# Norm weights folded into the rotation tables, and one reciprocal for both row sums of a query tile

## The chip, the cores and the metric

The kernel runs on one core of one Trainium2 chip. The metric is the device time of one execution in microseconds (us); smaller is better. A core has five engines, each of which works through its own instruction list in order: TensorE (PE in the profile, with PEld for its weight loads), VectorE (DVE), ScalarE (ACT), GpSimd (POOL) and SyncE (SP). DMA transfers are issued by an instruction on one of these lists and then run beside them.

## What is computed

The reference is a trunk of two layers. The first has MLA attention beside chunked retention, the second has differential attention beside bidirectional RWKV-7 time mixing; a gated ConvFFN follows each. 512 latent tokens and 128 context tokens go through it, 640 in all, with 256 cached context keys. The change touches only the second layer's differential attention, 4 heads with two maps each:

```python
q = rms_norm(dq.reshape(b, n, DIFF_HEADS, 2, DIFF_DH), qn)   # qn, kn: 64 weights each
k = rms_norm(dk.reshape(b, n, DIFF_HEADS, 2, DIFF_DH), kn)
q, k = apply_rope(q, cos, sin), apply_rope(k, cos, sin)      # latent tokens only
...
s = jnp.einsum('bqhcd,bkhcd->bchqk', qi, k) * scale          # scale = 0.125
p = jax.nn.softmax(s, axis=-1)
w = p[:, 0] - lam * p[:, 1]
o = jnp.einsum('bhqk,bkhe->bqhe', w, v)                      # then an rms_norm over each head
```

`rms_norm(x, g)` is x / sqrt(mean(x^2) + eps) * g, and `apply_rope` turns pairs of neighbouring columns by an angle that depends on the token. The normed k of the 128 context tokens, which are not rotated, is an output too.

## The kernel before

All five instruction lists are made ahead of the run by a scheduler: it takes the program in the order in which the Python code emits it, estimates how long each instruction takes, and puts the instructions of each engine into a fixed order by those estimates (L2112). An engine never overtakes: an instruction that waits holds everything behind it on its list. So a small change in the code can move rows that it does not name.

The stage that the change touches runs from about 1050 to 1510 us. There `rwkv_scan` (L1649) emits the RWKV work piece by piece and, in between, single steps of a background generator, `side_mix` (L1404); `weave` and `Side` (L211 and after) set how many steps go between two pieces, and tie a step's matmuls to earlier RWKV matmuls. The background generator runs two things in turn.

`odd_qkv` (L1266) projects q, k and v. Six groups of 256 columns (two for q, two for k, two for v) times five token tiles of 128 make 30 tiles; each takes 16 matmuls (L1326), after which ACT copies the result into `raw` (L1331) and, for q and k, squares it into `m` (L1334), and DVE sums the squares per head (L1335). PSUM has two `qkv` buffers. While one group is projected, `post` (L1278) of the group before it runs: for each tile, DVE multiplies `raw` by 1/rms (L1288, one operand is `y`, the result of the square root), POOL multiplies it by the norm weights (L1289, operand `rt`), DVE multiplies it by the cosine half of the rotation table into `m` (L1294), POOL by the sine half into another `m` (L1295), DVE adds the two into `raw` (L1298, two instructions), PE turns the tile (L1304, `qtr`), ACT and DVE split it into a high and a low part in the one `pt` buffer (L440, L444), and two DMAs write that to the arrays `dq` or `dk` (L1308). The fifth tile, the context, is not rotated. The table `ropd` (128 x 512, 256 KB) is loaded once, from ACT's list.

`diff_attn` (L1409) then takes the heads one by one. `load` (L1412) brings q, k and v of a head in with DMAs that POOL issues (L1424 to L1429, `aq`, `ak`, `ac`, `av`). `s1` (L1435) makes, for each of 5 query tiles and both maps, the scores on PE (L1442, `sc`), their maximum on DVE (L1445, `mx`) and the exponentials with their row sum on ACT (L1447, `p` and `sm`). From the two sums DVE makes two reciprocals (L1452 `rr`, L1453 `so`) and one product (L1454), and then the weights p0 + rr * p1 (L1455); dividing by p0's sum is put off. `s2` (L1459) turns the weights (L1466, copied by ACT at L1467), multiplies them with v (L1471), copies the result out (L1472) and squares it on ACT (L1473), which is scaled by `so` there. `finish` (L1476) norms a finished head.

Of the kernel before, what the change touches and what calls it, by code (L numbers as in the profile page):

```python
# [9 lines left out]
F32 = mybir.dt.float32  # L10
# [3 lines left out]
OP = mybir.AluOpType  # L14
# [248 lines left out]
class Trunk:  # L263
# [1002 lines left out]
    def odd_qkv(self, D):  # L1266

        nc, a = self.nc, self.a
        with self.pool("qk", 1, "left") as qp, self.psum("qps", 2) as qps, self.psum("qtr") as qtr:
            def tile(s, w, bufs, dt=F32):  # L1270
                return qp.tile([128, w], dt, name=self.nm(s), tag=s, bufs=bufs)

            nc.vector.tensor_scalar(self.row("dqn"), self.row("dqn"), 0.125, None, op0=OP.mult)
            rope = qp.tile([128, 2, 4, 64], F32, name="ropd")
            nc.scalar.dma_start(rope.rearrange("p a t d -> p (a t d)"), a["ropd"])
            h = self.x

            def post(g, raw, ms):  # L1278
                nc.vector.tensor_scalar(ms, ms, 1.0 / 64, EPS, op0=OP.mult, op1=OP.add)
                r = self.rsqrt(ms, 20)  # L1280
                yield
                name, gain = (("q", "dqn"), ("k", "dkn"))[g // 2]
                gain = self.row(gain)
                c0 = (g % 2) * 256
                for t in range(5):
                    q = raw[t]
                    qv = q.rearrange("p (h d) -> p h d", h=4)
                    nc.vector.tensor_tensor(qv, qv, r[:, t * 4:t * 4 + 4, None].to_broadcast([128, 4, 64]), op=OP.mult)  # L1288
                    nc.gpsimd.tensor_tensor(qv, qv, gain[:, None, :].to_broadcast([128, 4, 64]), op=OP.mult)  # L1289
                    yield  # L1290
                    if t < 4:
                        m1, m2 = tile("m", 256, 3), tile("m", 256, 3)
                        v1, v2 = (m.rearrange("p (h d) -> p h d", h=4) for m in (m1, m2))
                        nc.vector.tensor_tensor(v1, qv, rope[:, 0, t:t + 1, :].to_broadcast([128, 4, 64]), op=OP.mult)  # L1294
                        nc.gpsimd.tensor_tensor(v2, qv, rope[:, 1, t:t + 1, :].to_broadcast([128, 4, 64]), op=OP.mult)  # L1295
                        yield
                        for e in range(2):
                            nc.vector.tensor_tensor(q[:, e::2], m1[:, e::2], m2[:, 1 - e::2], op=OP.add)  # L1298
                    elif name == "k":
                        nc.sync.dma_start(a["dk_o"][:, c0:c0 + 256], q)  # L1300
                    yield
                    pt = qtr.tile([128, 512], F32, name=self.nm("qtr"), tag="tr")
                    for i in range(2):
                        nc.tensor.transpose(pt[:, i * 128:i * 128 + 128], q[:, i * 128:i * 128 + 128], self.ident)  # L1304
                    pts = tile("pt", 512, 1, F32R).rearrange("p (n x) -> p n x", n=2)
                    self.split_to(pts[:, 0], pts[:, 1], pt[:, :256])
                    for c in range(2):
                        nc.sync.dma_start(D[name][g % 2, c, :, :, t].rearrange("y d k -> d y k"),  # L1308
                                          pts[64 * c:64 * c + 64].bitcast(F32).rearrange("p n (h k) -> p (n h) k", h=2))
                    yield  # L1310

            def load(g):
                w = [tile("w", 1024, 3) for _ in range(2)]
                for i in range(2):
                    nc.sync.dma_start(w[i], a["wb_tm"][g][:, i * 1024:i * 1024 + 1024])
                return w

            w, pp = load(0), iter(())
            for g in range(6):
                wn = load(g + 1) if g < 5 else None  # L1320
                raw = []
                ms = self.S("ms", 20) if g < 4 else None
                for t in range(5):
                    ps = qps.tile([128, 512], F32, name=self.nm("qkv"), tag="ps")[:, :256]
                    for k in range(8):
                        nc.tensor.matmul(ps, h[k][:, t * 128:t * 128 + 128], w[k // 4][:, k % 4 * 256:k % 4 * 256 + 256], start=k == 0, stop=k == 7)  # L1326
                        if k % 2:
                            next(pp, None)
                            yield
                    r = tile("raw", 256, 6)  # L1330
                    nc.scalar.copy(r, ps)  # L1331
                    if g < 4:
                        sq = tile("m", 256, 3)
                        nc.scalar.activation(sq, ps, AF.Square)  # L1334
                        nc.vector.tensor_reduce(ms[:, t * 4:t * 4 + 4], sq.rearrange("p (h d) -> p h d", h=4), axis=AX.X, op=OP.add)  # L1335
                        raw.append(r)
                    else:
                        cs = slice((g - 4) * 256, (g - 4) * 256 + 256)
                        nc.sync.dma_start(D["v"][t][:, cs], r)
                        if t == 4:  # L1340
                            nc.sync.dma_start(a["dv_o"][:, cs], r)
                for _ in pp:
                    yield
                pp = post(g, raw, ms) if g < 4 else iter(())
                w = wn
            kc = tile("w", 1024, 3)
            ks = [tile("w", 1024, 3, F32R) for _ in range(2)]
            nc.sync.dma_start(kc, a["dkc"])
            self.split_to(*ks, kc)
            for i in range(2):  # L1350
                for c in range(2):
                    for g in range(2):
                        nc.sync.dma_start(D["k"][g, c, 2 * i:2 * i + 2, :, 5:7].rearrange("h d t k -> d h (t k)"),
                                          ks[i][64 * c:64 * c + 64, g * 512:g * 512 + 512].bitcast(F32).rearrange("p (h x) -> p h x", h=2))
            yield
# [53 lines left out]
    def diff_attn(self, D, ap, scp, trp):  # L1409
        nc, a = self.nc, self.a  # L1410
        nlam = self.diff_lam(ap)
# [23 lines left out]
        def s1(q, k, qt, so):  # L1435
            n = 768 if qt < 4 else 128
            pr = []
            for c in range(2):
                sc = scp.tile([128, 1024], F32, name=self.nm("sc"), tag="sc")
                for o, w, t0, t1 in ((0, 0, 0, 4), (512, 1, 0, 2)) if qt < 4 else ((0, 0, 4, 5),):  # L1440
                    for i in range(2):
                        nc.tensor.matmul(sc[:, o:o + (t1 - t0) * 128], q[c][i][:, qt].bitcast(F32R), k[c][w][:, t0:t1].bitcast(F32R), start=i == 0, stop=i == 1)  # L1442
                yield
                mx, sm = self.S("mx", 1), self.S("sm", 1)
                nc.vector.tensor_reduce(mx, sc[:, :n], axis=AX.X, op=OP.max, negate=True)  # L1445
                p = ap.tile([128, 768], F32, name=self.nm("p"), tag="p", bufs=4)[:, :n]
                nc.scalar.activation(p, sc[:, :n], AF.Exp, bias=mx, accum_out=sm)  # L1447
                pr.append((p, sm))
                yield
            (p0, m0), (p1, m1) = pr  # L1450
            r = self.S("rr", 1)
            nc.vector.reciprocal(r, m1)  # L1452
            nc.vector.reciprocal(so, m0)  # L1453
            nc.vector.scalar_tensor_tensor(r, r, nlam, m0, op0=OP.mult, op1=OP.mult)  # L1454
            nc.vector.scalar_tensor_tensor(p0, p1, r, p0, op0=OP.mult, op1=OP.add)  # L1455
            yield
            return p0
# [18 lines left out]
        def finish(h, o, so, ms):  # L1476
            nc.vector.tensor_scalar(ms, ms, 1.0 / 128, EPS, op0=OP.mult, op1=OP.add)
            f = self.rsqrt(ms, 5)
            nc.vector.tensor_tensor(f, f, so, op=OP.mult)
            yield  # L1480
            on = self.X("on")
            for t in range(5):
# [13 lines left out]
        prev = None  # L1496
        for h in range(4):
            q, k, v = load(h)
            o = self.X("ao").rearrange("p (t c) -> p t c", t=5)
            so, ms = self.S("so", 5, "so"), self.S("oms", 5, "oms")  # L1500
            yield
            for qt in range(5):
                w = yield from s1(q, k, qt, so[:, qt:qt + 1])
                if prev:
                    yield from s2(*prev[0])
                    if prev[1]:
                        yield from finish(*prev[1])
                prev = ((w, v, qt, o[:, qt], so[:, qt:qt + 1], ms[:, qt:qt + 1]), (h, o, so, ms) if qt == 4 else None)
        yield from s2(*prev[0])
        yield from finish(*prev[1])  # L1510

# [604 lines left out]
```

## Time and profile before

| | |
|---|---|
| median of 3 runs | 2064.08 us (2053.91 to 2064.95) |
| the profiled execution: its time | 2061.5 us |
| the profiled execution: its span | 2059.7 us, 36835 instructions |
| busy, share of the span | PE 95%, PEld 86%, DVE 61%, ACT 43%, POOL 9% |
| stage with the change | about 1050 to 1510 us of the span |

The profile is one execution. Its span runs from the first to the last instruction, and its time adds what lies around that. An engine's busy share is an average over stages that have different limits, so a stage is read by itself: which engine is busy in it, at what clock TensorE ran (1.00 in a window is full speed, 2.4 GHz; 0.50 is the lower level, 1.2 GHz), what each engine sat idle for, and the chain of waits, which is followed back from the last instruction to what released it.

### The profile page before, as it was taken

The page shows a single profiled execution, that of the slowest core. Times are in us where ns is not written, and L with a number is a line of the kernel's source. Part 1 is how long each engine was busy: PE and PEld are TensorE (multiplying, and loading weights), DVE is VectorE, ACT ScalarE, POOL GpSimd, SP SyncE. Part 2 cuts the span into 40 slices and gives each one's busy share as a digit, 9 for nine tenths or more (in the row PEclk, how much of TensorE's full clock was granted, in tenths as well). Part 3 has the DMA queues.
Part 4 walks back from the last instruction along what each step waited for, and adds up shares of the span by engine and source line. Part 5 has one row for each costly group of instructions (what it writes and reads, how often), then busy time and mean ns, then how long its engine had stood idle before and what let it go on. Part 6 is the DMA issues. An engine that isn't in the chain of part 4 may idle for free.

```text
span 2059.7 us, 36835 instructions
## 1 busy us (share of the span) xinstructions
PE 1965.6 (95%) x14696; PEld 1773.5 (86%) x14696; DVE 1252.0 (61%) x2666; ACT 880.0 (43%) x1669; POOL 184.9 (9%) x355
## 2 busy tenths in 40 slices
PE   6999999999999999999989898988879999999999
PEld 3998665999889899999978677767769999999999
DVE  6554567456446466577536856876667764656555
ACT  4343344344234243356334345655534542524343
POOL 1001000000000000000024332332110000000000
PEclk9999999999999999999999997898889999999999
DMA  8237343333553522244264464342453222222222
GB/s 323 67 109 237 93 142 117 134 103 124 174 178 113 189 71 75 72 132 137 76 221 116 112 184 121 109 114 69 120 182 106 76 59 93 60 85 67 77 63 71
DMA packets 162663, 245.62 MB, mean 119 GB/s; under 512 B 60154, under 2 KB 104314, under 8 KB 161212
## 3 DMA queue, kind: packets, MB, share of 16 engines
q1 hardware_dynamic: 156864, 227.84, 35.7%
q0 software_dynamic: 3904, 13.37, 2.3%
q8 instruction: 116, 1.90, 0.4%
q10 hardware_dynamic: 1724, 2.06, 0.4%
q14 instruction: 55, 0.45, 0.1%
HBM read 204.01 MB, written 39.21 MB: 118 GB/s over the span
## 4 chain that ended last, share of the span: by engine, by line
PE 84%; DVE 7%; DMA 5%; ACT 2%; issue 1%; SPq 0%; POOL 0%; ACTq 0%; DVEq 0%; POOLq 0%
PE mm L470 60%; PE qkv L1326 3%; PE ada L541 2%; PE rv L913 1%; PE pv L1130 1%; PE mm L1097 1%; PE ptr L1120 1%; PE sc L1442 1%; PE pv L1471 1%; DVE tmp L1907 1%; DVE X L1908 1%; PE ada L563 1%; DMA LI<-ld 1%; PE mm L1098 1%; DMA ld<-L 1%
## 5 line engine op out<-in xcount | busy, mean ns | idle before, releaser
L414 ACT CAST hi<-raw 128x1024 fp32r<-128x1024 f32 (+4 forms) x212 | 195.8, 925 | 570.3 <-PE mm L470 525.7
L470 PE MATMUL mm<-hhi,hi 128*128 128x322 f32 x1648 | 381.0, 312 | 0.0
L470 PE MATMUL mm<-hlo,hi 128*128 128x322 f32 x1648 | 380.3, 311 | 0.0
L470 PE MATMUL mm<-hhi,lo 128*128 128x322 f32 x1648 | 380.1, 311 | 0.0
L470 PEld LDWEIGHTS mm<-hhi,hi 128*128 128x128 f32 x1648 | 278.3, 189 | 8.7 <-issue 6.7
L470 PEld LDWEIGHTS mm<-hlo,hi 128*128 128x128 f32 x1648 | 279.5, 190 | 0.0
L470 PEld LDWEIGHTS mm<-hhi,lo 128*128 128x128 f32 x1648 | 278.6, 189 | 0.0
L415 DVE TENSOR_TENSOR lo<-raw,hi 128x1024 fp32r<-128x1024 f32 (+4 forms) x212 | 226.7, 1070 | 60.2 <-ACT hi L414 37.2
L672 DVE SCALAR_TENSOR_TENSOR x<-mm,ada,x 128x512 f32<-128x512 f32 (+1 forms) x176 | 88.8, 547 | 175.3 <-PE mm L470 175.2
L470 PE MATMUL mm<-ahi,hi 128*128 128x320 f32 x704 | 161.8, 311 | 0.0
L470 PE MATMUL mm<-ahi,lo 128*128 128x320 f32 x704 | 160.7, 309 | 0.0
L470 PE MATMUL mm<-alo,hi 128*128 128x320 f32 x704 | 160.3, 309 | 0.0
L663 DVE COPY shv<-mm 128x2 f32<-128x2 f32 x103 | 16.4, 159 | 206.3 <-PE mm L470 206.3
L470 PEld LDWEIGHTS mm<-ahi,hi 128*128 128x128 f32 x704 | 117.1, 188 | 12.0 <-ACT hi L414 10.1
L1326 PE MATMUL qkv<-w,x 128*128 128x256 f32 x480 | 115.6, 393 | 10.1 <-ACT m L1334 6.5
L470 PEld LDWEIGHTS mm<-alo,hi 128*128 128x128 f32 x704 | 117.7, 188 | 0.0
L470 PEld LDWEIGHTS mm<-ahi,lo 128*128 128x128 f32 x704 | 117.7, 188 | 0.0
L1326 PEld LDWEIGHTS qkv<-w,x 128*128 128x128 f32 x480 | 90.7, 195 | 28.4 <-ACT m L1334 8.6
L666 ACT ACTIVATE u<-u,shv 128x128 f32<-128x128 f32 (+1 forms) x176 | 90.4, 557 | 48.8 <-DVE u L665 47.0
L734 DVE SCALAR_TENSOR_TENSOR ac<-u,vt,ac 128x642 f32<-128x642 f32 x88 | 78.1, 888 | 52.4 <-ACT ac L732 52.1
L732 ACT ACTIVATE ac<-u,vt 128x642 f32<-128x642 f32 x88 | 81.3, 925 | 2.8
L665 DVE TENSOR_TENSOR u<-mm,rb 128x128 f32<-128x128 f32 (+1 forms) x176 | 77.4, 482 | 2.5 <-ACT rb L650 2.5
(422 smaller groups left out, 3363.7 us busy)
## 6 DMA issues: line engine op xcount, KB each, us to landing
raw<-ada SPq DMA_DIRECT2D x96, 512.0 KB, 4.6
raw<-up SPq DMA_DIRECT2D x88, 512.0 KB, 3.5
raw<-down SPq DMA_DIRECT2D x32, 384.0 KB, 3.4
fs<-df SPq DMA_DIRECT2D x10, 1088.0 KB, 6.7
raw<-down SPq DMA_DIRECT2D x32, 320.0 KB, 2.9
raw<-wb_fm SPq DMA_DIRECT2D x15, 512.0 KB, 3.7
w<-wb_tm SPq DMA_DIRECT2D x12, 512.0 KB, 5.3
raw<-wa_fm SPq DMA_DIRECT2D x11, 512.0 KB, 4.8
```

Of the source, the lines that this page charges most:

```text
L414: nc.scalar.copy(hi, t)
L415: nc.vector.tensor_tensor(lo, t, hi.bitcast(F32), op=OP.subtract)
L470: nc.tensor.matmul(ps[:, c0 + b:c0 + e], wt[:, ws], at[:, b:e], start=first and j == 0, stop=last and j == 2)
L541: nc.tensor.matmul(ps[32 * j:32 * j + 32, :], self.cs[:, k, :], pieces[j // 2][:, (j % 2) * 512:(j % 2) * 512 + 512], start=k == 0, stop=k ...
L563: nc.tensor.matmul(ps[32 * j:32 * j + 32, :], self.cs[:, k, :], p[:, j * 512:j * 512 + 512], start=k == 0, stop=k == 7, skip_group_check=True)
L665: nc.vector.tensor_tensor(u[:, o], ps[:, s], rb[:, s], op=OP.mult)
L666: nc.scalar.activation(u[:, o], u[:, o], AF.Identity, bias=sh[:, c:c + 1])
L672: nc.vector.scalar_tensor_tensor(x[:, s], ps[:, s], self.ada_v(l, part, m, c), x[:, s], op0=OP.mult, op1=OP.add)
L732: nc.scalar.activation(ac, u[:, 1:643], AF.Identity, scale=cv[:, 1, f:f + 1], bias=self.vec(f"cb{l}", f))
L734: nc.vector.scalar_tensor_tensor(ac, u[:, 0:642], cv[:, 0, f:f + 1], ac, op0=OP.mult, op1=OP.add)
L913: nc.tensor.matmul(ps[:, :272], at[:, ts], wt[:, k * 272:k * 272 + 272], start=n == 0, stop=n == 23)
L1326: nc.tensor.matmul(ps, h[k][:, t * 128:t * 128 + 128], w[k // 4][:, k % 4 * 256:k % 4 * 256 + 256], start=k == 0, stop=k == 7)
```

## The change

In `odd_qkv`, the norm weights are multiplied into the rotation table, once for q and, after the table has been loaded a second time into the same buffer, once for k. `post` then multiplies by the weights on POOL only for the context tile. In `s1`, both row sums go into two neighbouring columns of `so`; POOL multiplies the first with -lambda (`nlam`) before it is overwritten, one DVE reciprocal of two columns overwrites both, and one DVE product makes `rr`.

```diff
-            rope = qp.tile([128, 2, 4, 64], F32, name="ropd")
-            nc.scalar.dma_start(rope.rearrange("p a t d -> p (a t d)"), a["ropd"])
+            def tables(name):
+                t = tile("rope", 512, 1)
+                nc.scalar.dma_start(t, a["ropd"])
+                v = t.rearrange("p (x d) -> p x d", d=64)
+                nc.gpsimd.tensor_tensor(v, v, self.row(f"d{name}n")[:, None, :].to_broadcast([128, 8, 64]), op=OP.mult)
+                ropes[name] = t.rearrange("p (a t d) -> p a t d", a=2, t=4)
+
+            tables("q")
...
+                if g == 2:
+                    tables("k")
+                rope = ropes[name]
                 for t in range(5):
...
-                    nc.gpsimd.tensor_tensor(qv, qv, gain[:, None, :].to_broadcast([128, 4, 64]), op=OP.mult)
+                    if t == 4:
+                        nc.gpsimd.tensor_tensor(qv, qv, gain[:, None, :].to_broadcast([128, 4, 64]), op=OP.mult)
...
+                sm = so[:, c:c + 1]
...
-            r = self.S("rr", 1)
-            nc.vector.reciprocal(r, m1)
-            nc.vector.reciprocal(so, m0)
-            nc.vector.scalar_tensor_tensor(r, r, nlam, m0, op0=OP.mult, op1=OP.mult)
+            r, m0 = self.S("rr", 1), self.S("m0", 1)
+            nc.gpsimd.tensor_tensor(m0, so[:, 0:1], nlam, op=OP.mult)
+            nc.vector.reciprocal(so, so)
+            nc.vector.tensor_tensor(r, so[:, 1:2], m0, op=OP.mult)
             nc.vector.scalar_tensor_tensor(p0, p1, r, p0, op0=OP.mult, op1=OP.add)
```

The other lines of the diff pass `so` on as a tile of two columns per query tile. The number of steps that the background generator yields stays as it was, and so does the number of matmuls. DVE's list gets 20 instructions shorter (2668 to 2648), POOL's 6 longer (360 to 366). In the changed file the lines are other ones: L1280 is the table's multiplication, L1301 the context tile's, L1306 and L1307 are the products with the table, L1458 is `mx`, L1465 POOL's `m0` (written `m_` and a number), L1466 the reciprocal, L1467 `rr`, L1468 the weights.

The first place is POOL's list around the post of the second q group (`raw_10570` and after are its tiles, `hq` belongs to RWKV). Before:

```order
L1289 TENSOR_TENSOR raw_10570<-raw_10570,rt 128x256
L1289 TENSOR_TENSOR raw_10604<-raw_10604,rt 128x256
L1295 TENSOR_TENSOR m_10773<-raw_10570,ropd 128x256
L1289 TENSOR_TENSOR raw_10638<-raw_10638,rt 128x256
L1289 TENSOR_TENSOR raw_10679<-raw_10679,rt 128x256
L1289 TENSOR_TENSOR raw_10736<-raw_10736,rt 128x256
L1870 COPY hq_10890<-hq_10890 64x256 x2
L1295 TENSOR_TENSOR m_10825<-raw_10604,ropd 128x256
L1870 COPY hq_10977<-hq_10977 64x256
L1295 TENSOR_TENSOR m_10861<-raw_10638,ropd 128x256
L1870 COPY hq_10977<-hq_10977 64x256
L1295 TENSOR_TENSOR m_10904<-raw_10679,ropd 128x256
```

The same place after the change:

```order
L1307 TENSOR_TENSOR m_10769<-raw_10570,rope_10384 128x256
L1301 TENSOR_TENSOR raw_10733<-raw_10733,rt 128x256
L1307 TENSOR_TENSOR m_10820<-raw_10603,rope_10384 128x256
L1839 TENSOR_TENSOR th_10777<-kd_10778,fs_10366 128x512
L1307 TENSOR_TENSOR m_10855<-raw_10636,rope_10384 128x256
L1883 COPY hq_10883<-hq_10883 64x256 x2
L1307 TENSOR_TENSOR m_10897<-raw_10676,rope_10384 128x256
L1280 TENSOR_TENSOR rope_10983<-rope_10983,rt 128x512
L1883 COPY hq_10970<-hq_10970 64x256 x2
L1307 TENSOR_TENSOR m_10990<-raw_10788,rope_10983 128x256
```

Four of the five weight products are gone; the k table's product (`rope_10983`), which needs the table's second load, now stands ahead of two `hq` copies. That load stands on ACT's list right behind the third copy and square of the first k group.

The second place is DVE's list at one query tile of head 0 (its fourth; `so_11916` before and `so_11904` after are the row sums of that head). Before:

```order
L1453 RECIPROCAL so_11916<-sm_12175 128x1
L1445 TENSOR_REDUCE mx_12186<-sc_12181 128x1
L1452 RECIPROCAL rr_12199<-sm_12187 128x1
L1454 SCALAR_TENSOR_TENSOR rr_12199<-rr_12199,nlam,sm_12175 128x1
L1445 TENSOR_REDUCE mx_12237<-sc_12232 128x1
L1455 SCALAR_TENSOR_TENSOR p_12177<-p_12189,rr_12199,p_12177 128x768
```

After:

```order
L1458 TENSOR_REDUCE mx_12170<-sc_12165 128x1
L1466 RECIPROCAL so_11904<-so_11904 128x2
L1467 TENSOR_TENSOR rr_12182<-so_11904,m_12183 128x1
L1468 SCALAR_TENSOR_TENSOR p_12161<-p_12172,rr_12182,p_12161 128x768
L1458 TENSOR_REDUCE mx_12221<-sc_12216 128x1
```

The reciprocal between the two maxima, which waited for the first map's sum, has left DVE's list; the one that is left stands behind the second maximum and needs POOL's `m_12183` to have read the first sum.

The third place is POOL's list where head 1's operands are loaded while head 0 is worked on. Before:

```order
L1798 TENSOR_SCALAR lw_13072<-lw_13072 128x512
L1810 COPY pe_13090<-ex_10346 128x8
L1844 TENSOR_TENSOR kr_13130<-fs_12296,ex_10346 128x8x64
L1826 TENSOR_TENSOR th_13096<-kd_13097,fs_12296 128x512
L1428 DMA av_12325<-dv 128x5x128
L1429 DMA av_12325<-dvc 128x2x128
```

After:

```order
L1437 DMA ak_12314<-dk 64x640 x2
L1436 DMA aq_12310<-dq 64x640 x2
L1465 TENSOR_TENSOR m_12254<-so_11904,nlam 128x1
L1436 DMA aq_12312<-dq 64x640 x2
L1811 TENSOR_SCALAR lw_13049<-lw_13049 128x512
L1440 DMA av_12308<-dv 128x5x128
L1441 DMA av_12308<-dvc 128x2x128
L1823 COPY pe_13067<-ex_10346 128x8
L1857 TENSOR_TENSOR kr_13107<-fs_12279,ex_10346 128x8x64
L1465 TENSOR_TENSOR m_12384<-so_12333,nlam 128x1
```

`m_12254` (head 0, last tile) now stands behind DMA issues of the next head, and `m_12384` (head 1, first tile) behind RWKV's `lw`, `pe` and `kr` and behind the `av` loads, which have moved ahead of `pe`.

## Rows read from the trace of the kernel before

**Rows 1.** The page: shares of the engines in the chain that ended last.
```profile
PE 84%; DVE 7%; DMA 5%; ACT 2%; issue 1%; SPq 0%; POOL 0%; ACTq 0%; DVEq 0%; POOLq 0%
```

**Rows 2.** Stages: from:to, us, busy PE PEld DVE ACT POOL, clock, DMA share, GB/s.
```profile
1050.00:1230.00 180.00, 164.94 (x1092) 132.34 (x1094) 107.67 (x298) 67.10 (x179) 64.20 (x95) 0.97 0.54 153
1230.00:1510.00 280.00, 245.57 (x3176) 199.28 (x3174) 193.67 (x563) 159.98 (x419) 69.99 (x118) 0.85 0.44 117
```

**Rows 3.** Chain of waits from 1058 to 1510: shares by line; one of its pieces.
```profile
by line: PE qkv L1326 15.2%; PE sc L1442 5.2%; PE pv L1471 4.6%; DVE tmp L1907 4.3%; DVE X L1908 4.3%; issue 3.3%; DMA LI<-ld 3.0%; DMA ld<-L 2.8%; PE sb L1863 2.7%; ACT p L1447 2.2%; PE ptr L1466 2.2%; PE sa L1862 2.1%; DMA dk<-pt 2.1%; PE
...
1183.89 2.50 DMA dk<-pt
```

**Rows 4.** Instructions by line, 1050 to 1230: busy us, mean ns, idle before, releasers.
```profile
L1326 PE MATMUL qkv<-w,x 128*128 128x256 f32 x480 | 115.6, 393 | 10.1 <-ACT m L1334 6.5 <-ACT raw L1331 1.8 <-DMA w<-wb_tm 1.7
...
L1289 POOL TENSOR_TENSOR raw<-raw,rt 128x256 f32<-128x256 f32 x20 | 16.9, 868 | 12.3 <-DVE raw L1288 12.3
...
L1288 DVE TENSOR_TENSOR raw<-raw,y 128x256 f32<-128x256 f32 x20 | 13.0, 701 | 0.1
...
L440 ACT CAST pt<-qtr 128x256 fp32r<-128x256 f32 x20 | 7.5, 373 | 37.7 <-DMA dq<-pt 16.0 <-DMA dk<-pt 12.0 <-PE qtr L1304 9.7
```

**Rows 5.** Line L1288: durations in ns, min/median/max.
```profile
L1288 DVE TENSOR_TENSOR raw<-raw,y x20: 414/684/949, 1087.2 to 1189.0; 128x256 f32<-128x256 f32 x20
```

**Rows 6.** Windows of 10 us, columns as in rows 2.
```profile
1140.00:1150.00 10.00, 8.20 (x46) 6.29 (x45) 9.93 (x34) 3.25 (x11) 3.54 (x2) 1.00 0.40 123
1150.00:1160.00 10.00, 6.09 (x29) 5.04 (x28) 9.83 (x25) 2.27 (x6) 6.70 (x9) 0.83 0.43 128
...
1310.00:1320.00 10.00, 9.09 (x122) 7.12 (x117) 10.00 (x25) 5.65 (x15) 2.97 (x3) 1.00 0.52 147
...
1470.00:1480.00 10.00, 8.75 (x48) 7.20 (x49) 3.94 (x8) 3.71 (x11) 0.00 (x0) 0.52 0.34 88
```

**Rows 7.** POOL products of 128x512 elements, by line, 1050 to 1230.
```profile
L1826 POOL TENSOR_TENSOR th<-kd,fs 128x512 f32<-128x512 f32 x4 | 6.5, 1628 | 9.9 <-DVE kd L1823 9.8
...
L1844 POOL TENSOR_TENSOR kr<-fs,ex 128x512 f32<-128x512 f32 x4 | 5.6, 1409 | 0.0
```

**Rows 8.** The table's DMA (line L1275).
```profile
DMA to landing us min/median/max: 7.1/7.1/7.1
```

**Rows 9.** ACT's timeline: start, us, what; third and fourth copy of that k group.
```profile
1132.08 0.38 ACT L1331 COPY raw<-qkv 128x256 f32<-128x256 f32 x1
...
1138.44 0.38 ACT L1331 COPY raw<-qkv 128x256 f32<-128x256 f32 x1
```

**Rows 10.** Small instructions by line: durations in ns, min/median/max.
```profile
L1453 DVE RECIPROCAL so<-sm x20: 146/163/165, 1254.4 to 1485.4; 128x1 f32<-128x1 f32 x20
...
L1454 DVE SCALAR_TENSOR_TENSOR rr<-rr,nlam,sm x20: 205/219/1239, 1258.3 to 1489.0; 128x1 f32<-128x1 f32 x20
...
L1479 DVE TENSOR_TENSOR y<-y,so x4: 159/160/166, 1328.9 to 1505.1; 128x5 f32<-128x5 f32 x4
...
L1810 POOL COPY pe<-ex x10: 191/204/989, 1070.8 to 1412.7; 128x8 f32<-128x8 f32 x10
```

**Rows 11.** DVE's timeline: start, us, what, idle before it.
```profile
1254.40 0.16 DVE L1453 RECIPROCAL so<-sm 128x1 f32<-128x1 f32 x1 [4.31 <-ACT p L1447]
...
1485.37 0.16 DVE L1453 RECIPROCAL so<-sm 128x1 f32<-128x1 f32 x1 [0.56 <-ACT p L1447]
...
1488.78 0.17 DVE L1452 RECIPROCAL rr<-sm 128x1 f32<-128x1 f32 x1 [1.58 <-ACT p L1447]
```

**Rows 12.** PE's timeline, columns as in rows 11.
```profile
1254.43 1.22 PE L1442 MATMUL sc<-ak,aq 128*128 128x512 f32 x2 [2.81 <-ACT p L1447]
```

**Rows 13.** Waits from 1230 to 1510: us in total, times, longest.
```profile
POOL lw L1798 <- ACT lw L1796: 26.9, 5, 12.2
...
POOL av L1428 <- PE pv L1471: 22.4, 3, 11.8
...
DVE so L1453 <- ACT p L1447: 10.9, 10, 4.3
```

More of the change, by code (lines that the diff above doesn't have):

```diff
@@ L1273, in odd_qkv @@
             nc.vector.tensor_scalar(self.row("dqn"), self.row("dqn"), 0.125, None, op0=OP.mult)
-            rope = qp.tile([128, 2, 4, 64], F32, name="ropd")
-            nc.scalar.dma_start(rope.rearrange("p a t d -> p (a t d)"), a["ropd"])
+            ropes = {}
+            def tables(name):
[5 more added lines that the diff above has]
+            tables("q")
             h = self.x
@@ L1443, in s1 @@
                 yield
-                mx, sm = self.S("mx", 1), self.S("sm", 1)
+                mx = self.S("mx", 1)
                 nc.vector.tensor_reduce(mx, sc[:, :n], axis=AX.X, op=OP.max, negate=True)
@@ L1447, in s1 @@
                 nc.scalar.activation(p, sc[:, :n], AF.Exp, bias=mx, accum_out=sm)
-                pr.append((p, sm))
+                pr.append(p)
                 yield
-            (p0, m0), (p1, m1) = pr
-            r = self.S("rr", 1)
-            nc.vector.reciprocal(r, m1)
-            nc.vector.reciprocal(so, m0)
-            nc.vector.scalar_tensor_tensor(r, r, nlam, m0, op0=OP.mult, op1=OP.mult)
+            p0, p1 = pr
+            r, m0 = self.S("rr", 1), self.S("m0", 1)
+            nc.gpsimd.tensor_tensor(m0, so[:, 0:1], nlam, op=OP.mult)
+            nc.vector.reciprocal(so, so)
+            nc.vector.tensor_tensor(r, so[:, 1:2], m0, op=OP.mult)
             nc.vector.scalar_tensor_tensor(p0, p1, r, p0, op0=OP.mult, op1=OP.add)
@@ L1478, in finish @@
             f = self.rsqrt(ms, 5)
-            nc.vector.tensor_tensor(f, f, so, op=OP.mult)
+            nc.vector.tensor_tensor(f, f, so[:, :, 0], op=OP.mult)
             yield
@@ L1499, in diff_attn @@
             o = self.X("ao").rearrange("p (t c) -> p t c", t=5)
-            so, ms = self.S("so", 5, "so"), self.S("oms", 5, "oms")
+            so, ms = self.S("so", 10, "so").rearrange("p (t c) -> p t c", c=2), self.S("oms", 5, "oms")
             yield
             for qt in range(5):
-                w = yield from s1(q, k, qt, so[:, qt:qt + 1])
+                w = yield from s1(q, k, qt, so[:, qt])
                 if prev:
@@ L1507, in diff_attn @@
                         yield from finish(*prev[1])
-                prev = ((w, v, qt, o[:, qt], so[:, qt:qt + 1], ms[:, qt:qt + 1]), (h, o, so, ms) if qt == 4 else None)
+                prev = ((w, v, qt, o[:, qt], so[:, qt, 0:1], ms[:, qt:qt + 1]), (h, o, so, ms) if qt == 4 else None)
         yield from s2(*prev[0])
```

## The prediction

> **What bounds the kernel now.** I read the page's chain first: TensorE holds 84% of the chain that ended last, VectorE 7%, GpSimd nothing that shows [rows 1]. So an edit that takes no matmul away can only gain where TensorE waits. The table by stage says where that is. From 1050 to 1230 TensorE is busy 164.9 of 180 us at nearly full clock; from 1230 to 1510 it is busy 245.6 of 280 us, but at a mean clock of 0.85 [rows 2]. With two levels, 1.00 and 0.50, that mean means that about 0.30 x 280 = 84 us of the second stretch ran at the lower one. The chain through both stretches consists of many short pieces; the projection holds 15.2%, the scores and the products with v 5% each, and VectorE's solves for RWKV 4.3% twice [rows 3]. No one engine bounds the stage; it is a weave of two dependent streams, with VectorE full for some stretches (9.93 and 9.83 of 10 us in 1140 to 1160, 10.00 in 1310 to 1320) while TensorE sits partly idle (6.09 busy in 1150 to 1160) [rows 6].
>
> **Part 1, the weight products of q and k.** Sixteen of twenty leave GpSimd: 16 x 0.868 = 13.9 us of its list [rows 4]. GpSimd is busy 64 of 180 us there [rows 2], so this is worth nothing by itself. What matters is VectorE. Its product with 1/rms takes 414 ns at best, 949 at worst and 701 in the mean [rows 4, 5], and runs in batches of five beside GpSimd's weight products; I take the difference from the best to be what the two cost each other. That gives VectorE up to 20 x (0.701 - 0.414) = 5.7 us. Besides, the first tile of each group no longer has a weight product between its scaling and its rotation: 4 x 0.868 = 3.5 us of latency. Together the end on the gain's side is 9.2 us. The other end is nothing, since what holds ACT's split of the turned tiles is mostly the landing of the DMAs out of the one `pt` buffer, 16.0 + 12.0 us of its 37.7 us idle [rows 4], and that buffer does not change. In between I count VectorE's share for the one group of four that falls into the full stretch, 5.7 / 4 = 1.4 us, and the first tile's 0.87 us for the other three, 2.6: **-4**.
>
> The trace shows a slowdown of at most 949 - 414 = 535 ns beside products of 868 ns, never the whole of them [rows 4, 5]. The Trainium skill, "SBUF — State Buffer", section "SBUF: two separate sides", goes further: a VectorE instruction with two SBUF inputs and a GpSimd instruction that reads SBUF exclude each other, and the loser blocks until the other is done. By that a removed product could give VectorE back its full length; the case is the third rival below.
>
> **Part 2, the second table.** The first load and its product fall into a stretch in which nobody needs the table yet. The second load is issued by ACT behind its third copy of the first k group, and by then the last reader of q's table is normally done. The load takes between 2.5 us, like a tile's DMA [rows 3], and the 7.1 us of the first one [rows 8]; GpSimd's product takes 1.41 to 1.63 us [rows 7]; so the table is ready 3.9 to 8.7 us after the issue. Behind the product two `hq` copies of RWKV are queued on GpSimd, and ACT needs them right after its fourth copy, 1138.44 - 1132.08 = 6.4 us after the third [rows 9]. So the wait is 0 to 8.7 - 6.4 = 2.3 us. I take **0**, since the first load ran while the stage's big loads did, and the second runs among tile DMAs like the one of 2.5 us.
>
> **Part 3, the reciprocals.** Per query tile VectorE loses one reciprocal, 0.163 us, and its three-operand product of 0.219 becomes a plain one of about 0.160, going by the four-times-executed product of 5 columns [rows 10]. The two-column reciprocal costs as much as a one-column one, since these small instructions all take about 0.16. That is 0.222 x 20 = 4.4 us of VectorE. The bounds are 0 and -4.4. VectorE is busy 194 of 280 us in the stretch [rows 2], and I let the saving count by that share, 0.69 x 4.4: **-3**.
>
> A wait goes too. The early reciprocal made VectorE wait for the first map's exponential, 10.9 us in 10 waits [rows 13], once 4.31 us [rows 11]. But at that place TensorE waited for the same exponential, 2.81 us, before it could start the next scores [rows 12], which VectorE's next maximum needs. What is late next is therefore mostly the same thing. Bounds 0 and -10.9; I take **-1**, near the end that this row supports.
>
> **Part 4, GpSimd in the path of the weights.** The reciprocal overwrites the first sum, so it must wait until GpSimd has multiplied it by -lambda. Behind it on VectorE stand the weights of the tile, the next maximum and RWKV's solves; the score buffers and so TensorE wait for these. The product itself is short, by the nearest row 0.204 us [rows 10], and has a cover: from the first sum to the second one pass 1488.78 - 1485.37 = 3.4 us [rows 11]. But GpSimd's list has entries that wait long. Where a head changes, the product stands behind DMA issues, behind `av` loads that wait for the last product with the old v (22.4 us in three waits), and behind `lw` (longest 12.2 us) [rows 13]. If each of these were in the way, 22.4 - 3 x 3.4 = 12.2 us and 12.2 - 3.4 = 8.8 us would stand above the cover, 21.0 us in all. If the scheduler's order fits the run, nothing does. GpSimd is busy only 70 of 280 us here [rows 2], and 16 of the 20 products stand away from the head changes; I take a tenth of the far end, **+2**.
>
> That product's 0.204 us on GpSimd stands beside 0.160 us for one on VectorE [rows 10]. The Trainium skill, "GPSIMD Engine Reference", section 4.1 "Engine selection", advises against GpSimd for elementwise work, as about twice as slow with two inputs. On the path, uncovered, the row's 20 x 0.204 = 4.1 us would undo part 3, and the sum below would be about -2; the rows of the cover speak against that.
>
> **The sum.** -4 + 0 - 3 - 1 + 2 = **-6 us**. On the profiled execution's own time, 2061.5 us, that is 2055.5. This execution is 2.6 us below the median of the runs shown; on the median the forecast is 2064.1 - 6 = **2058 us**, -0.3%. A measurement of this kernel can tell about 0.5%, or 10.3 us, from no change, so this counts as the same.
>
> **The clock and the moved rows.** The new lists differ from the old ones in this whole stage, not only at the edited lines. TensorE's clock makes that expensive or cheap: after the idle 2.81 us at 1254, two score matmuls of 512 columns took 1.22 us, and the window from 1470 to 1480 ran at 0.52 with 8.75 us busy [rows 6, 12]. At full clock that window's work is about 4.4 us shorter. One such window more or fewer is 4.4 us, and the moved rows can make or close a gap of this kind anywhere. This has no sign that I can argue; I put two windows, 8.8 us, into the range on either side of the plainer cases.
>
> **Rivals.**
> 1. *Nothing reaches the end*: about 2064. The pt buffer's DMAs pace the post, TensorE is 92% busy in the first stretch [rows 2, 4], and the small instructions fall into VectorE's idle third. Against it: the windows in which VectorE is full [rows 6].
> 2. *Slower, by GpSimd's queue*: part 4 at its far end. The gains stay at -8, the waits cost 21: 2064 - 8 + 21 = 2077. It needs `av` to be issued ahead of the product while the old v is still read, as the new list has it in head 1. Waits above the cover turn the sign once they pass 8 us in all, and show as slower by 0.5% past 18 us.
> 3. *A larger gain*: VectorE was blocked for the whole of each removed product. Then part 1 is -13.9 instead of -4, and the sum -13.9 - 3 - 1 + 2 = -15.9: 2048. The same size results from the -6 and two half-clock windows fewer, -6 - 8.8 = -14.8. For it: VectorE's full windows; against the first form the 535 ns of at most.
>
> **How the numbers follow.** Forecast 0.38, nothing 0.20, slower 0.20, larger gain 0.22. Faster than 2053.8: most of the third rival, 0.20, and a tail of the forecast, 0.10. Slower than 2074.4: 0.14 of the second rival and 0.03 from unlucky clock windows in the other cases. The rest, 0.53, is the same. The low end of the range is the third rival less one window, 2048 - 4.4 = 2044; the high end is no gain, the late table's 2.3 and two windows more, 2064 + 2.3 + 8.8 = 2075.
>
> **What would show it.** Part 1: the product with 1/rms at some 420 ns in the mean, and the rotation's first product following it without a gap. Part 2: GpSimd's table product waiting for its DMA, and whether ACT's `hq` copies then wait for GpSimd. Part 3: 20 reciprocals fewer, none that waits for a first exponential. Part 4: VectorE's reciprocal released by ACT's exponential (cover holds) or by GpSimd's `m0` (cover gone). The clock: the granted clock of 1230 to 1510 against 0.85. The forecast is wrong if that clock moves by more than 0.03 (0.03 x 280, about 8 us), or if reciprocals wait for GpSimd for more than 8 us in all.

## The result

The changed kernel takes 2089.97 us (median of 4 runs, 2087.88 to 2091.25), the kernel before 2060.38 us beside it: a ratio of 1.0146, 95% interval 1.0113 to 1.0179, about 30 us slower. The forecast was 2058 us in a range of 2044 to 2075, so it was wrong in size and in sign.

First the whole span: TensorE's mean granted clock, before and then after, and the page's busy line, before and then after.

```profile
core 0: 2059.7 us, clock 0.969
```

```profile
core 0: 2087.8 us, clock 0.955
```

```profile
PE 1965.6 (95%) x14696; PEld 1773.5 (86%) x14696; DVE 1252.0 (61%) x2666; ACT 880.0 (43%) x1669; POOL 184.9 (9%) x355
```

```profile
PE 1983.6 (95%) x14696; PEld 1786.5 (86%) x14696; DVE 1246.6 (60%) x2646; ACT 882.9 (42%) x1669; POOL 181.1 (9%) x361
```

VectorE and GpSimd are less busy than before, ACT is 2.9 us busier. TensorE does the same 14696 matmuls, but is busy for 1983.6 instead of 1965.6 us. Of the 28.1 us by which the profiled span grew, 18.0 us are the same matmuls taking longer, and 10.1 us (104.2 against 94.1) are idle time of TensorE. And 2059.7 x 0.969 = 1995.8, 2087.8 x 0.955 = 1993.8: counted in full-speed time, idle time with it, both spans are the same to 2 us.

The stages of the changed kernel, in the columns of [rows 2], and below them four windows of 10 us:

```profile
1050.00:1230.00 180.00, 163.39 (x1015) 129.47 (x1014) 95.89 (x269) 64.50 (x171) 47.68 (x69) 0.92 0.50 148
1230.00:1510.00 280.00, 244.21 (x2926) 197.68 (x2924) 188.85 (x535) 151.72 (x386) 78.87 (x141) 0.79 0.38 103
...
1320.00:1330.00 10.00, 5.30 (x66) 4.24 (x64) 9.47 (x27) 5.78 (x18) 5.59 (x6) 0.88 0.38 99
1330.00:1340.00 10.00, 9.72 (x75) 7.89 (x75) 8.97 (x31) 3.33 (x9) 0.82 (x3) 0.50 0.33 113
1340.00:1350.00 10.00, 10.00 (x56) 8.02 (x56) 8.27 (x27) 5.21 (x11) 0.92 (x3) 0.50 0.09 33
1350.00:1360.00 10.00, 10.00 (x68) 7.17 (x67) 2.99 (x7) 6.15 (x15) 3.17 (x8) 0.50 0.25 54
```

The clock fell from 0.97 to 0.92 in the first stretch and from 0.85 to 0.79 in the second. By the two levels that is 2 x 0.05 x 180 + 2 x 0.06 x 280 = 52 us more at half speed, which is 26 us of full-speed time. The largest single piece stands from about 1326 to 1362 us. TensorE's timeline at its start:

```profile
1323.66 0.68 PE L2017 MATMUL yp<-hq,SV 64*64 64x64 f32 x14
1325.62 0.72 PE L1455 MATMUL sc<-ak,aq 128*128 128x512 f32 x2 [1.29 <-ACT p L1460]
1326.18 0.40 PE L1455 MATMUL sc<-ac,aq 128*128 128x256 f32 x2
1330.28 0.66 PE L1842 MATMUL bp<-th,rkb 128*32 128x128 f32 x8 [3.70 <-POOL th L1839]
```

After 3.70 us of waiting for GpSimd's `th`, the 8 small `bp` matmuls take 0.66 us, where the same 8 took 0.42 at full clock (shown further down). `th` itself was waiting for VectorE's `kd`, which stood in a full stretch of VectorE's list (9.47 of 10 us). (The profile's row of `th`, shown at the end, names the reciprocal `so`, since that ended last. But `th` does not read `so`; it starts 0.150 us after the end of `kd` here, and 0.144 to 0.155 us after it wherever it waited in this kernel.) None of `bp`, `th` and `kd` was edited.

The edited instructions did roughly what the prediction said. Two lines of the projection stretch (1050 to 1230) with the shortest, median and longest of the first one, then GpSimd's new product and VectorE's reciprocal over the whole span:

```profile
L1299 DVE TENSOR_TENSOR raw<-raw,y 128x256 f32<-128x256 f32 x20 | 9.4, 531 | 0.1
...
L1299 DVE TENSOR_TENSOR raw<-raw,y x20: 409/418/949, 1087.5 to 1182.5; 128x256 f32<-128x256 f32 x20
...
L1280 POOL TENSOR_TENSOR rope<-rope,rt 128x512 f32<-128x512 f32 x2 | 2.5, 1272 | 8.5 <-DMA rope<-ropd 8.5
```

```profile
L1465 POOL TENSOR_TENSOR m<-so,nlam 128x1 f32<-128x1 f32 x20 | 4.7, 237 | 41.0 <-ACT p L1460 40.6
L1466 DVE RECIPROCAL so<-so 128x2 f32<-128x2 f32 x20 | 3.3, 163 | 11.6 <-ACT p L1460 11.6
```

VectorE's product with 1/rms (L1299) is at 531 ns in the mean, against 701 in [rows 4]. Fifteen of the twenty now take 409 to 424 ns. The third tile of each group still takes 945 to 949, beside GpSimd's rotation product (L1307), which the change leaves in place, and one tile takes 616. The two-column reciprocal costs 163 ns like the one-column ones of [rows 10]; and what VectorE waits for there, in this kernel, is ACT's exponential and never GpSimd. What looks bad is GpSimd's product: 40.6 us of waiting for the exponential, with RWKV's rows queued behind it. That was my first suspect.

### The profile page after: what moved, and what is told of

Its sections match the earlier page's. It is cut to its first block, busy times and chain, and to the rows that moved or that the text cites. A ratio compares the mean times of both kernels' runs of the same rounds, so it can differ in the third digit from the quotient of the medians.

```text
span 2087.8 us, 36802 instructions
## 1 busy us (share of the span) xinstructions
PE 1983.6 (95%) x14696; PEld 1786.5 (86%) x14696; DVE 1246.6 (60%) x2646; ACT 882.9 (42%) x1669; POOL 181.1 (9%) x361
## 5 line engine op out<-in xcount | busy, mean ns | idle before, releaser
L1338 PE MATMUL qkv<-w,x 128*128 128x256 f32 x480 | 122.7, 406 | 6.1 <-ACT m L1346 3.8
L470 PEld LDWEIGHTS mm<-ahi,hi 128*128 128x128 f32 x704 | 117.0, 188 | 12.0 <-ACT hi L414 10.1
```

The lines of the kernel that those rows point to most:

```text
L470: nc.tensor.matmul(ps[:, c0 + b:c0 + e], wt[:, ws], at[:, b:e], start=first and j == 0, stop=last and j == 2)
```

## The experiments

Two theories. **Order**: the scheduler put the rows of the lists into another order, TensorE's above all, and this order has more gaps after which TensorE runs at the lower clock; the edits themselves cost nothing. **Queue**: the edits cost, because GpSimd's product waits for the exponential and holds up what is queued behind it, or because the second table does.

Order and work can be taken apart, since the scheduler honours edges that only fix an order on one engine (they add no wait). A list of instruction numbers in the wanted order is put into the kernel file, and behind the traced program:

```diff
     with tile.TileContext(nc, schedule_with_timeline_sim=True) as tc:
         trunk(tc, a)
+        _pin(tc)
...
+def _pin(tc):
+    by = {i.name: i for i in tc.nc.cur_bb.bb.instructions}
+    for s in _ORDER:                      # one list for each pinned engine
...
+        for x, y in zip(seq, seq[1:]):
+            tc.add_manual_dep(by[f"I-{y}"], f"I-{x}", mybir.DependencyInfo(mybir.DependencyClass.NoSync, ...), reason="pinned")
```

Rows that only one of the two kernels has are left to the scheduler.

**The change's work in the order before** (all five engines pinned).

> The change's whole work, but every row that both kernels have stands on its engine's list exactly where it stood before the change (order-only edges between neighbours, no waits); the 20 GpSimd products, the tables' products and the second load of the table stand where the scheduler put them between these. Theory order (the new order of rows costs the time, through TensorE's low clock; the edited instructions cost nothing): 0.994 to 1.003 of the kernel before, granted clock near 0.969, and waits of GpSimd for the exponential may stay as they are. Theory queue (GpSimd's product waits for the exponential and holds up RWKV's rows behind it, or the table's load does): 1.010 or more, as the changed kernel.

Measured: 0.9976 of the kernel before, 0.9949 to 1.0002. The profile's granted clock is 0.970.

**The work before in the changed order.**

> The work of the kernel before, nothing edited, but every row that both kernels have stands in the changed kernel's order; the 16 weight products and the 20 early reciprocals stand where the scheduler put them. Theory order: 1.010 to 1.022 of the kernel before, granted clock 0.950 to 0.960. Theory queue: within 0.5% of the kernel before, since there is no GpSimd product in the weights' path and no second table.

Measured: 1.0174, 1.0131 to 1.0217. Nothing of the change is in this kernel, and it loses as much as the change or more. The queue theory falls with these two. The waits it rested on are still there in the kernel that lost nothing; waits of `p_after_in_before` from 1230 to 1510 (total us, times, longest):

```profile
POOL m L1465 <- ACT p L1460: 37.2, 5, 10.0
...
DVE so L1466 <- POOL m L1465: 3.0, 2, 1.5
```

In the same stretch the changed kernel's product waited for 32.7 of its 40.6 us. So 37 us of GpSimd standing still cost nothing that shows, nor did the 3.0 us for which VectorE's reciprocal waited for GpSimd here.

**Each half alone, scheduler free.** The halves are the hunks of the diff in `odd_qkv` and those in `diff_attn`.

> The change's first half alone (weights in the tables, second load, 16 weight products fewer); s1 as before; the scheduler free. 1770 TensorE rows stand elsewhere than before, by up to 144 places, about as in the whole change (1744, up to 127). Theory order: 1.005 to 1.020, with most of the whole change's loss. Theory queue with the loss in the weights' path: within 0.5% of the kernel before. My terms for this half, without any cost of order: 0.998.

Measured: 1.0118, 1.0076 to 1.0161.

> The change's second half alone (one reciprocal for both sums, GpSimd's product); tables as before; the scheduler free. Only 528 TensorE rows stand elsewhere, by up to 41 places. Theory order: the less moves, the less can be lost, 0.997 to 1.006. Theory queue: 1.008 or more. My terms for this half, without any cost of order: 0.999.

Measured: 1.0018, 0.9989 to 1.0047. The half that moves many rows loses, the half that moves few doesn't.

**TensorE's list alone.** First the change's work with only this list pinned, then the work before with only this list in the changed order.

> The change's whole work, TensorE's list alone pinned to the order before; the other four lists are the scheduler's. If TensorE's order is what costs: 0.994 to 1.004. If it is the order of the other lists (GpSimd's, VectorE's): above 1.008.

Measured: 0.9960, 0.9938 to 0.9981 (2054.11 us against 2061.95). This one is faster than both kernels.

> The work of the kernel before, nothing edited, TensorE's list alone pinned to the changed kernel's order. If TensorE's order is the loss: 1.010 to 1.020, like the kernel before with all five lists in the changed order (1.0174). If the other lists share it: 1.003 to 1.009.

Measured: 1.0210, 1.0172 to 1.0248. To impose this one list is enough, in both directions: it takes the whole loss away, or brings it. That does not mean that the other lists have no share. The scheduler was free with them and fitted them to TensorE's: counted in the traces as rows outside the longest common order, ACT's list in `p_pe_only` is 11 rows of 1669 away from the kernel before and 138 from the changed one, VectorE's 101 and 275 of 2646. In the opposite kernel ACT's list is 133 rows away from the kernel before and 18 from the changed one. No run parts TensorE's order from the orders that come with it.

**Each half with TensorE's list in the order before.**

> The change's first half alone (tables), TensorE's list pinned to the order before, the other lists free. The same work with a free order took 1.0118. If TensorE's order is the whole loss, what is left is the prediction's term of this half, -4 us: 0.996 to 1.000. If the half itself costs (table load, GpSimd's table product): 1.005 or more.

Measured: 0.9979, 0.9959 to 0.9998.

> The change's second half alone (s1), TensorE's list pinned to the order before. The prediction's terms for this half are -3 - 1 + 2 = -2 us: 0.997 to 1.001. If GpSimd's product holds up VectorE or RWKV: 1.003 or more.

Measured: 0.9991, 0.9964 to 1.0017. In the same order of matmuls the tables gain about 4 us (by the interval 0.4 to 8), and the reciprocals 2 us or nothing; both together, above, 8.

**Neutral reorderings.** No instruction differs from the kernel before. In the first, two lines are swapped:

```diff
-                        nc.vector.tensor_tensor(v1, qv, rope[:, 0, t:t + 1, :]..., op=OP.mult)
                         nc.gpsimd.tensor_tensor(v2, qv, rope[:, 1, t:t + 1, :]..., op=OP.mult)
+                        nc.vector.tensor_tensor(v1, qv, rope[:, 0, t:t + 1, :]..., op=OP.mult)
```

> A neutral control: the kernel before, in which the two products of a rotation (VectorE's with the cosine half, GpSimd's with the sine half) are written in the other order. No instruction is added, removed or changed, but the scheduler moves 1168 TensorE rows by up to 79 places. Theory order, strong form (any reordering of this size costs or gains by the clock, the kernel before being a lucky order): 1.004 to 1.020. If only the changed kernel's order is bad, for a reason of its own: within 0.5%.

Measured: 1.0050, 1.0024 to 1.0075. In the second, the pace table differs:

```diff
-BG = (89, 24, 102, 0, 22, 72, 0)
+BG = (87, 24, 102, 0, 24, 72, 0)
```

> A second neutral control: the kernel before with two of its background steps handed out in a later stretch (the pace table's first number 87 for 89, its fifth 24 for 22). The same instructions; 1245 TensorE rows move, by up to 84 places, about as in the first control, which took 1.0050. If any such reordering costs: 1.003 to 1.015. If the first control was chance: 0.997 to 1.003, or below 1.

Measured: 1.0024, 0.9996 to 1.0052. The first shows a cost of order with no work behind it; the second leaves it open, as its interval holds 1. Both are smaller than what the change's order costs, with about two thirds as many rows moved.

**Half of the order.** What is emitted ahead of the first head's loads stands in the order before, the rest in the changed one.

> The change's whole work; what is emitted ahead of the first head's loads (projection, posts and RWKV's first pieces) stands in the order before, the rest in the changed kernel's order. The changed kernel lost about 10 us by 1230 us of the span and 15 more between 1290 and 1340. If the two losses are separate: 1.005 to 1.010 (the second one stays). If the second follows from the first: 0.996 to 1.004. If the first part's order has nothing to do with it: 1.012 to 1.018.

Measured: 1.0075, 1.0047 to 1.0103. Counted from the kernel before, half of the loss stays; counted from the changed work in the order before (0.9960), 0.0115 of 0.0186, somewhat more than half. So the two losses are separate. TensorE's list here is only 183 rows away from the changed kernel's (647 from the one before), so a small part of the moved rows goes with nearly half of the loss. The opposite half was not run.

**Filling gaps.** To see whether the clock carries the loss, idle matmuls keep TensorE busy where the changed kernel waits. Their results are overwritten, so nothing is left out; work is only added.

```diff
-        bp = self.PS("bp")[:, :128]
+        bp = self.PS("bp")
+        self.nbp = getattr(self, "nbp", -1) + 1
+        for i in range(FILL_BP.get(self.nbp, 0)):
+            nc.tensor.matmul(bp[:, 0:384], self.ident, self.c2[:, 0:384], start=True, stop=True)
+        bp = bp[:, :128]
```

with FILL_BP = {6: 10}, and all lists pinned to the changed kernel's own order.

> The changed kernel in its own order, with ten idle matmuls (128 x 384, of constants, into a PSUM tile that is overwritten right after) put ahead of RWKV's seventh bp, the place at 1326 to 1330 us where TensorE sat idle for 3.70 us waiting for GpSimd's th and then ran at the lower clock until about 1362. If the clock carries the loss: the windows from 1330 to 1360 at 1.00 instead of 0.50, and 1.005 to 1.010 of the kernel before (15 us less than the changed kernel). If the low clock only accompanies a loss that has another cause: 1.014 or more, ten matmuls longer.

Measured: 1.0123, 1.0091 to 1.0156, which can't be told from the changed kernel's 1.0146. Its windows, to be held against those of the changed kernel above, and the place itself:

```profile
1320.00:1330.00 10.00, 8.71 (x70) 6.00 (x66) 10.00 (x24) 4.65 (x13) 4.27 (x4) 1.00 0.42 103
1330.00:1340.00 10.00, 10.00 (x108) 7.56 (x107) 8.38 (x33) 4.27 (x9) 0.98 (x3) 1.00 0.25 103
1340.00:1350.00 10.00, 7.77 (x56) 5.88 (x55) 8.45 (x25) 6.66 (x17) 0.80 (x2) 0.79 0.17 61
```

```profile
1324.73 6.61 PE L1849 MATMUL bp<-c,ident 128*128 128x384 f32 x20
1331.27 0.42 PE L1852 MATMUL bp<-th,rkb 128*32 128x128 f32 x8
```

The clock did hold: 1.00 from 1330 to 1340 instead of 0.50, and `bp` takes 0.42 us instead of 0.66. But the fillers (two rows each) took 6.6 us in a gap of 3.7, and from 1342 on TensorE stood idle again. The same fillers, sized to the gaps, in three places (FILL_BP = {3: 3, 5: 2, 6: 6}):

> The changed kernel in its own order again, the idle matmuls now sized to the gaps and put into three of them: three ahead of RWKV's fourth bp (1.89 us of idle TensorE at 1204 in the changed kernel), two ahead of the sixth (1.17 us at 1286), six ahead of the seventh (3.70 us at 1330). If the gaps cost through the clock: windows behind 1204, 1290 and 1330 that ran at 0.50 run higher, and 1.003 to 1.009 of the kernel before, clearly under the 1.0123 of one oversized filler. If filling one gap only moves the low clock to the next: 1.010 to 1.015.

Measured: 1.0089, 1.0072 to 1.0105. The last bound lies under the changed kernel's lowest, 1.0113. Work was added and nothing taken away, and the kernel got faster than the changed one, by the ratios some 12 us (1.0146 - 1.0089 = 0.0057). The two profiles give less. Their spans differ by 11.3 us, but 4.4 of these are there ahead of the first filler, at the first copy of the projection, in the changed kernel and in this one:

```profile
1064.86 0.37 ACT L1343 COPY raw<-qkv 128x256 f32<-128x256 f32 x1 [4.31 <-PE qkv L1338]
```

```profile
1060.49 0.37 ACT L1349 COPY raw<-qkv 128x256 f32<-128x256 f32 x1 [4.55 <-PE qkv L1344]
```

That leaves some 7 us. So the fillers do gain; how much, between 7 and 12 us, isn't settled. Stretches of 30 us with the columns of [rows 2], first of the changed kernel, then of this one:

```profile
1190.00:1220.00 30.00, 25.29 (x105) 18.70 (x104) 8.01 (x13) 7.39 (x19) 5.15 (x9) 0.72 0.52 148
...
1280.00:1310.00 30.00, 27.27 (x341) 23.41 (x341) 17.71 (x34) 16.27 (x43) 9.77 (x18) 0.77 0.48 129
1310.00:1340.00 30.00, 24.37 (x292) 19.57 (x284) 26.49 (x87) 15.36 (x43) 9.63 (x14) 0.79 0.38 109
1340.00:1370.00 30.00, 29.80 (x217) 23.73 (x217) 16.59 (x43) 17.26 (x41) 8.43 (x17) 0.64 0.21 53
1370.00:1400.00 30.00, 25.05 (x360) 19.43 (x358) 18.64 (x59) 17.58 (x48) 10.15 (x19) 0.87 0.54 149
```

```profile
1190.00:1220.00 30.00, 26.48 (x280) 19.53 (x280) 10.00 (x17) 12.66 (x34) 5.51 (x9) 0.89 0.58 158
...
1280.00:1310.00 30.00, 28.64 (x349) 23.95 (x349) 16.30 (x44) 18.50 (x50) 9.88 (x20) 0.77 0.52 141
1310.00:1340.00 30.00, 27.36 (x265) 21.26 (x265) 28.59 (x89) 16.61 (x43) 7.65 (x10) 0.89 0.27 83
1340.00:1370.00 30.00, 27.37 (x266) 21.87 (x265) 16.82 (x37) 18.33 (x49) 14.55 (x27) 0.88 0.56 147
1370.00:1400.00 30.00, 26.22 (x327) 19.85 (x325) 20.81 (x64) 16.41 (x44) 6.88 (x10) 0.63 0.21 54
```

Around the first and the third filled place the clock rises from 0.72 to 0.89, from 0.79 to 0.89 and from 0.64 to 0.88. At the second, from 1280 to 1310, it stays at 0.77, so that part of the expectation failed. Behind them, from 1370 on, it falls to 0.63, where it was 0.87. So part of what a filled gap gives back is lost at the next one.

All profiles together, in us (idle is span less TensorE's busy time; full is span x clock):

| kernel | TensorE's order | span | busy | idle | clock | full |
|---|---|---|---|---|---|---|
| before | before | 2059.7 | 1965.6 | 94.1 | 0.969 | 1996 |
| p_after_in_before | before | 2049.5 | 1960.9 | 88.6 | 0.970 | 1988 |
| p_pe_only | before | 2053.4 | 1964.0 | 89.4 | 0.970 | 1992 |
| e_tables_pe | before | 2049.7 | 1968.1 | 81.6 | 0.968 | 1984 |
| e_s1_pe | before | 2054.0 | 1963.9 | 90.1 | 0.969 | 1990 |
| the change | its own | 2087.8 | 1983.6 | 104.2 | 0.955 | 1994 |
| p_before_in_after | the change's | 2097.6 | 1987.3 | 110.3 | 0.953 | 1999 |
| p_before_pe_after | the change's | 2104.8 | 1995.3 | 109.5 | 0.948 | 1995 |
| e_tables | its own | 2080.3 | 1971.5 | 108.8 | 0.960 | 1997 |
| e_s1 | its own | 2054.0 | 1960.4 | 93.6 | 0.970 | 1992 |
| n_swap | its own | 2072.5 | 1980.2 | 92.3 | 0.956 | 1981 |
| n_pace | its own | 2067.3 | 1973.1 | 94.2 | 0.963 | 1991 |
| h_proj_before | mixed | 2081.0 | 1977.7 | 103.3 | 0.960 | 1998 |
| f_fill | the change's | 2088.0 | 1985.5 | 102.5 | 0.958 | 2000 |
| f_fill2 | the change's | 2076.5 | 1978.4 | 98.1 | 0.962 | 1998 |

The spans lie 55 us apart, the full-speed time 19 us. Some 8 us of the span are not the change's: a ScalarE instruction that stands ahead of the stage in all 15 kernels, behind the same rows, starts between 995.9 and 1004.2 us. With the order before, the clock of these profiles is 0.968 to 0.970 whatever the work; with the change's order it is at most 0.955, unless gaps are filled. The runs that the ratios rest on spread more: 0.957 to 0.976 with the order before, 0.946 to 0.957 with the change's order and no filler. In `n_swap` TensorE is idle no longer than in the kernel before (92.3 against 94.1 us) and busy 14.6 us longer: in this profile its loss lies in the clock alone.

## Why the prediction was wrong, point by point

**Part 1, -4 us: right in size.** The tables alone, with the matmuls in the order before, measure 0.9979 (0.9959 to 0.9998), about -4 us. The means behind it were a little off: VectorE's product went to 531 ns in the mean and not to some 420, which is 20 x (0.701 - 0.531) = 3.4 us of VectorE instead of 5.7. The prediction took every product to be freed; 15 of 20 are at 409 to 424 ns, but four still meet GpSimd's rotation product.

**Part 2, 0 us: not contradicted.** GpSimd's two table products waited 8.5 us for their loads, and the half with them still gained.

**Part 3 and 4, together -2 us: not contradicted.** 0.9991, 0.9964 to 1.0017. The cover of 3.4 us held in the changed kernel: VectorE waited 11.6 us for the exponential and not once for GpSimd's product; in `p_after_in_before` it did so twice, for 3.0 us, under the 8 us that the prediction set as a sign. The wait for the first exponential did go: VectorE's waits for exponentials fall from 19.6 us (10.9 and 8.7) to 9.7 in `p_after_in_before`, and yet this half gains 2 us or nothing, as the prediction had argued. The second rival, GpSimd's queue, gave the right sign and less than half of the distance from no change (+13 against +30), and its mechanism is refuted by the two pinned kernels. Its 2077 us stood above the range's own high end, 2075.

**The sum, -6 us: right for the work.** 0.9976 and 0.9960 in the order before stand for -5 and -8 us. The first rival, that nothing reaches the end, is told against by the second of these, whose interval, 0.9938 to 0.9981, lies under 1; the first one's, 0.9949 to 1.0002, just holds 1.

**The step that failed** is "The clock and the moved rows". I saw that the whole stage was reordered, that TensorE's clock falls after gaps, and I knew the price of one window, 4.4 us. Then I gave the term no sign and two windows, 8.8 us. It measured 1.0146 - 0.9960 = 0.0186, some 38 us: four times as much, and all on one side. The term also priced the lower clock only, and the new waits themselves at nothing: of the 28.1 us by which the profiled span grew, 18.0 are longer matmuls and 10.1 are more idle time. The prediction's own sign of being wrong came: the clock from 1230 to 1510 moved by 0.06, twice the 0.03 that it named. One thing could have been read ahead of time, the number of rows that moved: 1744 of TensorE's, by up to 127 places, in a stage where half-clock time already made up 84 of 280 us; two windows were no bound for that. The sign could not be read; it took runs. Each of the five free reorderings that were run (the change, each half, the two controls) came out slower in its median than its work in the order before; for three of them the intervals are clear, for two not, and the change and its first half are nearly one order (304 of TensorE's rows apart, against 819 from the kernel before). So the kernel before seems to stand at the good end of what its scheduler gives. Why it does isn't shown by any run.

Where the loss arises is shown in halves only. At 1133 us RWKV's third `lw` still came 11 us ahead of the projection's fifteenth copy; in the changed order it comes 9 us behind it. ACT's timeline, before and after:

```profile
1133.26 0.60 ACT L1796 ACTIVATE lw<-wp 128x512 f32<-128x512 f32 x1
...
1144.18 0.38 ACT L1331 COPY raw<-qkv 128x256 f32<-128x256 f32 x1
```

```profile
1136.39 0.37 ACT L1343 COPY raw<-qkv 128x256 f32<-128x256 f32 x1 [1.68 <-PE qtr L1316]
...
1145.68 0.62 ACT L1809 ACTIVATE lw<-wp 128x512 f32<-128x512 f32 x1
```

The projection ran ahead (by 1190 us 392 of its 480 matmuls had started, against 365 before), RWKV fell behind, and between 1195 and 1205 TensorE waited in turn for a weight load (1.29 us), a `pt` tile (1.54) and `th` (1.89). `h_proj_before` confirms that this part's order costs up to half; that these very gaps do is argued from the timeline, and supported by the fillers. Which rows of TensorE's list matter, how the loss divides between waits and clock, and why the scheduler thought the new order good, stays open.

## What to carry to other kernels

Where a scheduler orders all engines, a small edit is two changes: the work, and a new order of everything near it. Compare the lists first, and measure the work with TensorE's list held in the old order; here that turned a loss of 1.5% into a gain of 0.4%, and nothing else of the change had to be altered. An engine's long wait in the profile (GpSimd's 40 us) is no cause until a kernel that keeps it loses too.

## What the runs showed of the hardware

- Added work made a kernel faster: eleven idle matmuls, 8.9 us of TensorE, took 7 to 12 us off the changed kernel (1.0146 to 1.0089). The granted clock around two of the three filled places rose (0.72 to 0.89, 0.64 to 0.88).
- A small VectorE instruction can be held until a GpSimd product ends. While `th` stood on GpSimd for 2.52 us, a VectorE instruction on 128 x 5 elements, which took 0.15 us at 1323.52, took 1.24 us and ended with it (1330.26 against 1330.23). `th` was long too: the shortest of its ten takes 1.29 us. VectorE's other instructions beside it took their usual time, so it looks as if `th` was held first and held VectorE then. GpSimd's and then VectorE's timeline of the changed kernel:

```profile
1327.71 2.52 POOL L1839 TENSOR_TENSOR th<-kd,fs 128x512 f32<-128x512 f32 x1 [4.27 <-DVE so L1466]
```

```profile
1323.52 0.15 DVE L482 SCALAR_TENSOR_TENSOR nt<-nt,oms 128x5 f32<-128x5 f32 x1
...
1329.02 1.24 DVE L482 SCALAR_TENSOR_TENSOR nt<-nt,oms 128x5 f32<-128x5 f32 x1
```

By the Trainium skill, "SBUF — State Buffer", section "SBUF: two separate sides", the loser of such a pair blocks until the other is done; this row agrees. The third rival, which rested on it, still didn't come about: the removed products gave VectorE's product 3.4 us and not 13.9. Of its 20 instances 13 were longer than 600 ns before, by 0.53 us at most over the shortest, and 5 still are.
